# Compressed-branch scores: both parts of the keys as one 32-column operand, token tiles in two turns

## The chip, the cores and the metric

The kernel runs on one core of one Trainium2 chip. The metric is the device time of one execution in microseconds (us). The kernel before was timed three times: 971.80, 973.91 and 974.85 us, median 973.91.

## The reference, cut to what matters

The reference is a model of two layers over 256 tokens of width 1024. Each layer has an attention part of two branches (A: dilated attention of 24 heads; B: attention of 8 query heads over 2 key heads in three ways) and a convolutional feed-forward part. The change touches one of the three ways of branch B, the attention over compressed keys:

```python
k_cmp = compress(b_kv[:, :, 0, 0], cmp_pos[l, 0], cmp_w1[l, 0], cmp_w2[l, 0])
k_cmp = apply_rope(rmsnorm(k_cmp, b_k_g[l, 0]), cos_c, sin_c)
...
s = jnp.einsum('bqhgd,bchd->bqhgc', qb, k_cmp, preferred_element_type=jnp.float32) * scale
valid = (cmp_end[None, :] <= t[:, None])[None, :, None, None, :]
s_m = jnp.where(valid, s, NEG)
m = jnp.max(s_m, axis=-1, keepdims=True)
e = jnp.where(valid, jnp.exp(s_m - m), 0.0)
p = e / jnp.maximum(jnp.sum(e, axis=-1, keepdims=True), TINY)
o_cmp = jnp.einsum('bqhgc,bchd->bqhgd', p.astype(v_cmp.dtype), v_cmp)
...
o = g[:, :, 0] * o_cmp + g[:, :, 1] * o_sel + g[:, :, 2] * o_win
```

Every query head has at most 16 compressed keys, so the scores of all 8 heads for one tile of 128 tokens are a 128x128 matrix.

## The kernel before, in words

The 256 tokens stand in two tiles of 128. All matmuls of the large projections are done in three passes on operands split into a high and a low part (`hi` and `lo`, both `float32r`): `hi`x`hi`, `hi`x`lo`, `lo`x`hi` (`mm3`, L289 to L292). The weights come from memory as a stream of units; for each half of a unit, SP loads `raw` (L208), ScalarE rounds it to `hi` (L238), and VectorE subtracts to get `lo` (L239). `hi` and `lo` have two buffers each, `raw` has five. So a 512-column matmul of L290 or L291 needs L238, and one of L292 needs L239.

In a layer's attention part the main stream on TensorE are the nine chunks of the A projection (`chunk_in`, L445) and eight units of the merge gates (`merge`, L948). After each group of 12 chunk matmuls (four k steps of three passes for one token tile) stands a `tick()` (L274): a turn, in which every side job that is under way goes on to its next `yield`. Side jobs are `job_a` (attention of branch A, four times), `job_b` (selected and window attention of branch B, eight times) and `job_cmp1` and `job_cmp2` (compressed keys and attention). So the program's order is: 12 wide matmuls, one step of every side job, 12 wide matmuls, and so on. The tile framework plans the order on each engine from this: an instruction that is ready can be placed ahead of earlier ones that wait. What stands on an engine in the end is seen in the trace, not in the text of the program.

`job_cmp2` (L836) starts when the last quarter of the hidden units is summed (in chunk 5). It makes the compressed keys, transposes them (L879) and splits them to `kf[:, 0]` and `kf[:, 1]`, the high and the low part (L881). In its next turn it takes one of four `pt` buffers (L885) and one of five PSUM tiles (L886) and does the scores (L887 to L892): for each of two token tiles and 8 heads two matmuls, one for either part of the keys, accumulated in PSUM. The stationary operand is the queries `qS[:, h % 2, h // 2, tok]` (128x128, high and low part on the partitions), the moving one 16 columns of `kf`. So each pair loads the same queries twice.

In the same turn VectorE adds the mask while it reads PSUM (L896), scales (L898), and the softmax follows (L900 to L910, its exponential on ScalarE, L902). A turn later the probabilities are transposed (L914) and the `pt` buffer is given back, then L926 multiplies with the values, L930 adds to the branch's sum, and the result `oTb` is the operand of the projection of branch B (L993), which comes after all chunks and four merge units.

L571 and L576 in the trace are `job_a`: products of probabilities and values (`col_pair`, 64 columns of the array each) and transposes of probabilities (`transposed`). L706 and L614 are its work on VectorE. L864 is `job_cmp2`'s second compression product, L957 to L959 are the matmuls of `merge`.

Of the kernel before, what the change touches and what calls it, by code (L numbers as in the profile page):

```python
# [15 lines left out]
ALU = mybir.AluOpType  # L16
# [3 lines left out]
P = 128  # L20
# [144 lines left out]
def block_kernel(ctx, tc, x_in, xo_in, ws, g_norm, g_rope, pos, w2, conv, rope_c, ropec_c, mask_c, misc_c, out):  # L165
    nc = tc.nc
    V, A, G, T = nc.vector, nc.scalar, nc.gpsimd, nc.tensor
# [5 lines left out]
    def acc():  # L173
        t = acc_p.tile([P, 512], F32, name="acc")
        return t

    def att():
        t = att_p.tile([P, 512], F32, name="att")
        return t
# [14 lines left out]
    cmask = misc[:, 0:32].rearrange("p (t c) -> p t c", t=2)  # L194
# [180 lines left out]
    def attention_layer(l, pool, hT):  # L375
# [26 lines left out]
        qS = pool.tile([P, 2, 4, S], F32R, name="qS")  # L402
# [181 lines left out]
        def take(tag, n):  # L584
            while free[tag] < n:
                yield
            free[tag] -= n
# [227 lines left out]
        def w1_unit(w):  # L815
            while len(Fc) < 2:
                tick()
            if w == 0:
                hps["ps"] = att()
            ps = hps["ps"]  # L820
            for jp, half in enumerate(next_unit()):
                wv = half.rearrange("p (u v n) -> p u v n", u=2, v=2)
                for kv in range(2):
                    for u in range(2):
                        r = 64 * kv + 32 * u
                        jj = 4 * w + 2 * jp + u
                        T.matmul(ps[r:r + 32, 0:256], hps["F"][:, kv, jj].rearrange("p h c -> p (h c)"), wv[:, u, kv],
                                 start=jj < 2, stop=jj >= 14)
            if w < 3:
                return  # L830
            hid = pool.tile([P, 256], F32, name="hid", bufs=1)
            A.copy(hid, ps[:, 0:256])
            hps["hid"] = hid
            side.appendleft(job_cmp2())

        def job_cmp2():  # L836
            while ready["b"] < 6:
                yield
            ps = att()
# [21 lines left out]
            ps = att()  # L861
# [16 lines left out]
            ps = att()  # L878
            T.transpose(ps[:, :P], t1.rearrange("p a d -> p (a d)"), ident)  # L879
            kf = pool.tile([P, 2, P], F32R, name="kf", tag="hid", bufs=1)  # L880
# [3 lines left out]
            yield  # L884
            yield from take("pt", 1)  # L885
            ps = att()  # L886
            for t in range(2):  # L887
                tok = slice(t * P, (t + 1) * P)
                for h in range(8):
                    for i in range(2):  # L890
                        T.matmul(ps[:, t * P + h * 16:t * P + h * 16 + 16], qS[:, h % 2, h // 2, tok],
                                 kf[:, i, h * 16:(h + 1) * 16], start=i == 0, stop=i == 1)  # L892
            es = pool.tile([P, 16, 16], F32, name="es", tag="pt", bufs=4)
            e4 = es.rearrange("p (t h) c -> p t h c", t=2)
            for t in range(2):
                V.tensor_tensor(e4[:, t], ps[:, t * P:(t + 1) * P].rearrange("p (h c) -> p h c", h=8),  # L896
                                cmask[:, t, None, :].to_broadcast([P, 8, 16]), op=ALU.add)
            V.tensor_tensor(es, es, qscB.rearrange("p t h -> p (t h)")[:, :, None].to_broadcast([P, 16, 16]), op=ALU.mult)  # L898
            sm = pool.tile([P, 3, 16], F32, name="sm")
            V.tensor_reduce(sm[:, 0], es, axis=AX.X, op=ALU.max)  # L900
# [21 lines left out]
            for i in range(2):  # L922
                p3 = att()
                for j in range(2):
                    hp = 2 * i + j
                    T.matmul(p3[:, j * S:(j + 1) * S], vcb[:, 2 * hp:2 * hp + 2].rearrange("p h d -> p (h d)"), eT,  # L926
                             start=True, stop=True)
# [45 lines left out]
        for ab in "ba":  # L973
# [3 lines left out]
            for u in range(2):  # L977
# [9 lines left out]
                for mp in range(2):  # L987
                    ps = acc()
# [168 lines left out]
```

## Time and profile before

| what | value |
|---|---|
| three runs | 971.80, 973.91, 974.85 us |
| the profiled execution | 974.93 us, of which the span of the trace is 973.1 |
| TensorE matmul row (PE) | 949.1 us busy, 98% |
| TensorE weight loads (PEld) | 860.4 us, 88% |
| VectorE (DVE) | 753.5 us, 77% |
| ScalarE (ACT) | 580.7 us, 60% |
| GpSimd (POOL) | 156.4 us, 16% |
| mean granted TensorE clock | 0.992 |
| read from memory | 163.69 MB, 169 GB/s over the span |

Times in the rows are microseconds from the span's start, if not marked as ns. A matmul's duration in the trace holds its way through the pipeline; what a matmul costs in a dense stream is the distance from one start to the next. The granted clock is the share of TensorE's full clock (1.00 is 2.4 GHz, 0.50 is 1.2 GHz). L891 is a line of the program, and "acc<-lo,hT" says which tiles an instruction writes and reads.

### The profile page before, as it was taken

How to read it: one execution, taken by the hardware profiler on the slowest of the kernel's cores; microseconds unless marked ns; L12 is line 12 of the kernel's file. 1: busy time of each engine (PE TensorE's matmuls, PEld its weight loads, DVE VectorE, ACT ScalarE, POOL GpSimd, SP SyncE). 2: the span in 40 equal slices, each digit the busy share in tenths (PEclk: the TensorE clock that was granted, in tenths of full speed). 3: DMA queues.
4: the chain of work that ended last, by engine and by line, in shares of the span. 5: the costliest groups of instructions: out<-in, count | busy, mean ns of one | idle time of the engine just before them, and what ended most of it. 6: DMA issues, size and time to landing. Idle time of an engine off the chain costs nothing.

```text
span 973.1 us, 18637 instructions
## 1 busy us (share of the span) xinstructions
PE 949.1 (98%) x7154; PEld 860.4 (88%) x7154; DVE 753.5 (77%) x1593; ACT 580.7 (60%) x1186; POOL 156.4 (16%) x179
## 2 busy tenths in 40 slices
PE   6899999999999999999998999999999999999998
PEld 4778887878999999999986787877799999999998
DVE  6898866778669898986478987677876888998742
ACT  5778665667546555555456886565756565555431
POOL 5140211212003111110122301121300111111100
PEclk9999999999999999999999999999999999999999
DMA  7734447424456566565455344554354465666660
GB/s 234 258 132 153 152 152 219 172 87 143 146 173 213 175 202 201 182 195 199 160 166 174 111 150 135 197 189 131 106 195 150 148 229 173 197 196 197 200 209 22
DMA packets 48041, 165.95 MB, mean 171 GB/s; under 512 B 6096, under 2 KB 7632, under 8 KB 47824
## 3 DMA queue, kind: packets, MB, share of 16 engines
q1 hardware_dynamic: 46800, 163.71, 51.3%
q8 instruction: 56, 0.92, 0.4%
q10 hardware_dynamic: 1152, 1.05, 0.3%
q14 instruction: 33, 0.27, 0.1%
HBM read 163.69 MB, written 1.05 MB: 169 GB/s over the span
## 4 chain that ended last, share of the span: by engine, by line
PE 80%; DVE 10%; ACT 6%; issue 2%; DMA 1%; POOL 1%; SPq 0%; DVEq 0%; ACTq 0%; POOLq 0%
PE acc L373 25%; PE acc L290 6%; PE acc L292 6%; PE acc L291 6%; PE acc L1084 4%; DVE lo L239 4%; PE acc L1083 4%; PE acc L1082 4%; PE att L571 3%; PE acc L957 3%; PE acc L959 3%; PE acc L958 3%; PE att L576 2%; ACT pt L664 2%; PE acc L993 2%
## 5 line engine op out<-in xcount | busy, mean ns | idle before, releaser
L239 DVE TENSOR_TENSOR lo<-raw,hi 128x1024 fp32r<-128x1024 f32 (+1 forms) x292 | 368.0, 1278 | 54.7 <-ACT hi L238 51.7
L238 ACT CAST hi<-raw 128x1024 fp32r<-128x1024 f32 (+1 forms) x292 | 293.8, 1037 | 161.1 <-PE acc L291 41.3
L373 PE MATMUL acc<-u,hi 128*128 128x256 f32 x1376 | 237.7, 278 | 0.0
L373 PEld LDWEIGHTS acc<-u,hi 128*128 128x128 f32 x1376 | 208.2, 188 | 0.1
L373 PE MATMUL acc<-u,lo 128*128 128x256 f32 x688 | 190.9, 277 | 0.0
L290 PE MATMUL acc<-hi,hT 128*128 128x512 f32 (+1 forms) x384 | 156.1, 406 | 8.1 <-ACT hi L238 8.1
L292 PE MATMUL acc<-lo,hT 128*128 128x512 f32 (+1 forms) x384 | 152.3, 397 | 4.9 <-DVE lo L239 4.8
L291 PE MATMUL acc<-hi,hT 128*128 128x512 f32 (+1 forms) x384 | 150.1, 391 | 0.0
L373 PEld LDWEIGHTS acc<-u,lo 128*128 128x128 f32 x688 | 129.3, 188 | 0.0
L1083 PE MATMUL acc<-act,hi 128*128 128x256 f32 x352 | 97.4, 277 | 0.0
L1084 PE MATMUL acc<-act,lo 128*128 128x256 f32 x352 | 97.4, 277 | 0.0
L1082 PE MATMUL acc<-act,hi 128*128 128x256 f32 x352 | 97.3, 277 | 0.0
L290 PEld LDWEIGHTS acc<-hi,hT 128*128 128x128 f32 x384 | 74.0, 193 | 26.1 <-ACT hi L238 10.2
L292 PEld LDWEIGHTS acc<-lo,hT 128*128 128x128 f32 x384 | 73.9, 192 | 24.2 <-DVE lo L239 9.4
L291 PEld LDWEIGHTS acc<-hi,hT 128*128 128x128 f32 x384 | 74.2, 193 | 12.8 <-issue 0.3
L957 PE MATMUL acc<-hT,hi 128*128 128x256 f32 x256 | 73.3, 286 | 0.0
L959 PE MATMUL acc<-hT,lo 128*128 128x256 f32 x256 | 71.8, 280 | 0.2 <-DVE lo L239 0.2
L958 PE MATMUL acc<-hT,hi 128*128 128x256 f32 x256 | 71.7, 280 | 0.0
L1084 PEld LDWEIGHTS acc<-act,lo 128*128 128x128 f32 x352 | 66.1, 188 | 0.0
L1082 PEld LDWEIGHTS acc<-act,hi 128*128 128x128 f32 x352 | 66.1, 188 | 0.0
L1083 PEld LDWEIGHTS acc<-act,hi 128*128 128x128 f32 x352 | 66.1, 188 | 0.0
L1054 POOL TENSOR_TENSOR z<-z,rb 128x512 f32<-128x512 f32 x22 | 30.4, 1384 | 204.7 <-DVE z L1053 204.7
(214 smaller groups left out, 1705.4 us busy)
## 6 DMA issues: line engine op xcount, KB each, us to landing
raw<-in_ws_dram SPq DMA_DIRECT2D x300, 512.0 KB, 4.6
raw<-in_ws_dram SPq DMA_DIRECT2D x8, 280.0 KB, 4.6
x<-in_x_dram SPq DMA_DIRECT2D x1, 1024.0 KB, 9.5
out_dram<-x ACTq DMA_DIRECT2D x8, 128.0 KB, 2.4
gr<-in_g_rope_dram SPq DMA_DIRECT2D x2, 384.0 KB, 4.7
masks<-in_mask_dram SPq DMA_DIRECT2D x1, 576.0 KB, 7.5
xo<-in_xo_dram SPq DMA_DIRECT2D x2, 256.0 KB, 4.6
xo<-in_xo_dram SPq DMA_DIRECT2D x1, 512.0 KB, 7.5
```

Source lines behind the costliest of these rows:

```text
L238: A.copy(h, r)
L239: V.tensor_sub(l, r, h.bitcast(F32))
L290: T.matmul(o, a_hi, b_hi, start=first, stop=False)
L291: T.matmul(o, a_lo, b_hi, start=False, stop=False)
L292: T.matmul(o, a_hi, b_lo, start=False, stop=last)
L373: return [lambda a=a: T.matmul(a[0], a[1], a[2], start=a[3], stop=a[4]) for a in todo]
L957: T.matmul(o, hi[:, k, ms], hT[:, 0, k], start=k == 0, stop=False)
L958: T.matmul(o, hi[:, k, ms], hT[:, 1, k], start=False, stop=False)
L959: T.matmul(o, lo[:, k, ms], hT[:, 0, k], start=False, stop=k == 7)
L1082: T.matmul(ps, hi[:, c], act[:, 0, k], start=k == 0, stop=False)
L1083: T.matmul(ps, hi[:, c], act[:, 1, k], start=False, stop=False)
L1084: T.matmul(ps, lo[:, c], act[:, 0, k], start=False, stop=k == NFT - 1)
```

## The change

The two matmuls of a head become one: the moving operand is both parts of the keys, 2x16 columns, and the results land in two halves of the PSUM tile instead of being accumulated. After each token tile's eight matmuls the job yields, so that the score matmuls stand in two turns and the work of VectorE on them in a third. VectorE adds the second half in an instruction of its own.

```diff
             ps = att()
+            pv = ps.rearrange("p (i t h c) -> p i t h c", i=2, t=2, h=8)
             for t in range(2):
                 tok = slice(t * P, (t + 1) * P)
                 for h in range(8):
-                    for i in range(2):
-                        T.matmul(ps[:, t * P + h * 16:t * P + h * 16 + 16], qS[:, h % 2, h // 2, tok],
-                                 kf[:, i, h * 16:(h + 1) * 16], start=i == 0, stop=i == 1)
+                    T.matmul(pv[:, :, t, h], qS[:, h % 2, h // 2, tok], kf[:, :, h * 16:(h + 1) * 16], start=True, stop=True)
+                yield
             es = pool.tile([P, 16, 16], F32, name="es", tag="pt", bufs=4)
             e4 = es.rearrange("p (t h) c -> p t h c", t=2)
             for t in range(2):
-                V.tensor_tensor(e4[:, t], ps[:, t * P:(t + 1) * P].rearrange("p (h c) -> p h c", h=8),
-                                cmask[:, t, None, :].to_broadcast([P, 8, 16]), op=ALU.add)
+                V.tensor_tensor(e4[:, t], pv[:, 0, t], cmask[:, t, None, :].to_broadcast([P, 8, 16]), op=ALU.add)
+            V.tensor_tensor(e4, e4, pv[:, 1], op=ALU.add)
```

## Rows read from the trace of the kernel before

**Rows 1.** The page, part 1: busy time, share and instructions of each engine.

```profile
PE 949.1 (98%) x7154; PEld 860.4 (88%) x7154; DVE 753.5 (77%) x1593; ACT 580.7 (60%) x1186; POOL 156.4 (16%) x179
```

**Rows 2.** Windows: stretch and its length, then columns as the head line says.

```profile
core 0: us, PE busy (x) PEld busy (x) DVE busy (x) ACT busy (x) POOL busy (x), PEclk, DMA share, GB/s
176.60:187.50 10.90, 10.52 (x67) 8.13 (x66) 10.31 (x22) 7.74 (x17) 3.36 (x4) 1.00 0.57 189
...
187.50:209.70 22.20, 22.20 (x118) 18.18 (x116) 15.39 (x43) 9.26 (x25) 1.77 (x2) 0.85 0.28 94
...
190.46:197.27 6.81, 6.81 (x29) 5.69 (x29) 4.00 (x12) 0.83 (x2) 0.00 (x0) 0.50 0.31 116
...
671.74:675.14 3.40, 3.40 (x16) 2.59 (x13) 2.66 (x8) 0.68 (x2) 0.00 (x0) 0.50 0.37 127
...
197.30:232.00 34.70, 34.46 (x189) 26.98 (x189) 27.62 (x86) 25.07 (x67) 9.23 (x11) 1.00 0.30 105
```

**Rows 3.** Line L891: its matmuls (ns min/median/max), and who waited for it.

```profile
L891 PE MATMUL att<-kf,qS x64: 255/257/363, 187.6 to 671.2; 128*128 128x16 f32 x64
...
  DVE es L896: 5.0, 2
```

**Rows 4.** Timeline of layer 0: start us, us, engine, line, what, [idle before].

```profile
186.84 2.35 DVE L239 TENSOR_TENSOR lo<-raw,hi 128x1024 fp32r<-128x1024 f32 x2
...
187.59 4.38 PE L891 MATMUL att<-kf,qS 128*128 128x16 f32 x32
...
191.90 1.55 PE L571 MATMUL att<-pT,vA 128*64 128x128 f32 x12
192.01 0.49 DVE L896 TENSOR_TENSOR es<-att,misc 128x128 f32<-128x128 f32 x2 [2.82 <-PE att L891]
...
193.38 0.80 PE L292 MATMUL acc<-lo,hT 128*128 128x512 f32 x1
...
197.57 0.39 PE L290 MATMUL acc<-hi,hT 128*128 128x512 f32 x1
...
200.10 0.39 PE L292 MATMUL acc<-lo,hT 128*128 128x512 f32 x1
...
200.49 0.41 PE L914 MATMUL att<-ident,es 128*128 128x128 f32 x2
```

**Rows 5.** Timeline of layer 1, the same place.

```profile
667.74 3.72 PE L891 MATMUL att<-kf,qS 128*128 128x16 f32 x32
...
676.16 0.40 PE L290 MATMUL acc<-hi,hT 128*128 128x512 f32 x1
```

**Rows 6.** Timeline of TensorE in other places of layer 0, at full clock.

```profile
227.14 1.09 PE L571 MATMUL att<-pT,vA 128*64 128x256 f32 x12
228.16 0.88 PE L576 MATMUL att<-ident,pt 128*128 128x128 f32 x6
228.79 0.48 PE L290 MATMUL acc<-hi,hT 128*128 128x512 f32 x1
229.10 0.39 PE L291 MATMUL acc<-hi,hT 128*128 128x512 f32 x1
...
179.64 1.04 PE L864 MATMUL att<-w2t,hr 128*128 128x64 f32 x8
...
171.69 0.28 PE L958 MATMUL acc<-hT,hi 128*128 128x256 f32 x1
...
172.72 0.28 PE L958 MATMUL acc<-hT,hi 128*128 128x256 f32 x1
```

**Rows 7.** Lines L896 and L706 on VectorE, ns min/median/max.

```profile
L896 DVE TENSOR_TENSOR es<-att,misc x4: 279/286/292, 192.0 to 671.7; 128x128 f32<-128x128 f32 x4
...
L706 DVE TENSOR_TENSOR res<-att,sc x8: 413/420/426, 143.6 to 753.2; 128x256 f32<-128x256 f32 x8
```

**Rows 8.** Timeline: the first matmul of branch B's projection in layer 0.

```profile
232.53 0.39 PE L993 MATMUL acc<-oTb,hi 128*128 128x256 f32 x1
```

**Rows 9.** Waits of TensorE from 20 to 330: us in total, times, longest.

```profile
PE acc L292 <- DVE lo L239: 3.4, 4, 2.2
```

## The prediction

> **What bounds the kernel now.** I read the busy shares first. TensorE's matmul row is busy for 98% of the span, VectorE for 77%, ScalarE for 60% [rows 1]. A row near 100% is not proof, since matmul ends are modelled, so I went on to start-to-start distances in the timeline: outside the places named below, TensorE starts its 512-column matmuls every 0.230 us for tens of us (from 197.57 to 200.10 are 11 distances) [rows 4]. The kernel is bound by TensorE's instruction stream, and VectorE's `lo` parts of the weights follow close behind.
>
> Then I asked where the changed line stands. It is 64 matmuls in all, 32 a layer, each 128x16 with a full 128x128 weight load of its own [rows 3]. In the timeline of layer 0 they start at 187.59 and the next thing (L571) at 191.90; VectorE stands 2.82 us at L896 for them [rows 4], 5.0 us in both layers [rows 3]. The stretches show more: the granted clock is 0.50, the lower of the two levels (1.2 instead of 2.4 GHz), from 190.46 to 197.27 and from 671.74 to 675.14, and 1.00 afterwards [rows 2]. What TensorE did just before either fall is this block of 16-column matmuls. After the fall the ten distances from the 512-column L292 at 193.38 to 197.57 take 4.19 us, 0.42 each, against 0.230 at full clock [rows 4]. So the block costs twice: by its loads, and by the half clock of the useful matmuls behind it.
>
> **The change part by part.**
>
> *Matmuls.* 32 a layer become 16, with 32 columns each. Distance now: 0.112 us (L891's 32 cover 4.38 us in layer 0, the end of them slowed, and 3.72 in layer 1: (3.72 - 0.26)/31 = 0.112) [rows 3, 5]. No row has 32 columns with this load. Eight matmuls of 64 columns (L864) cover 1.04 us, 0.11 each, and nine distances of 256-column matmuls with the same load (L957 to L959) take 1.03 us, 0.114 each [rows 6]. From 16 to 256 columns the distance is the same, so the load sets it; between 0.11 and 0.114 I take 0.112, 16 x 0.112 = 1.79 us a layer. That a wider operand makes it less than 0.11 is excluded by the same rows.
>
> *The block and what follows, at full clock.* Layer 0 now: from 187.59 to the L290 at 197.57, 9.98 us [rows 4]. The same work with 16 matmuls and the clock at 1.00: 1.79, then L571 x12 in 1.02 (227.14 to the next start at 228.16), then the ten distances of 512-column matmuls, the first at 0.31 (228.79 to 229.10) and nine at 0.230, 2.38 [rows 6]. Sum 5.19, saved 4.79. Layer 1 now: 667.74 to 676.16, 8.42 us [rows 5], saved 3.23. Together 8.02 us, of which 3.58 is the 32 matmuls fewer and 4.44 the clock. The second turn costs two more resumptions of the 512-column stream at some 0.1 (0.31 against 0.23): 0.2. Left 7.8.
>
> *Does the clock stay up?* The change leaves 16 instead of 32 thin matmuls and means to put ordinary ones between the two eights. But the order on TensorE is not the program's: in layer 0 the L571 of the same turn, and L891, stand ahead of ten 512-column matmuls of the turn before, which waited for the `lo` that VectorE makes from 186.84 to 189.19 [rows 4]. The eights of both turns could be pulled together in the same way. Even then the thin stretch is 1.8 us, while the clock fell 2.9 us (layer 0) and 4.0 us (layer 1) after the block's start [rows 2, 4, 5]. I take it that the clock holds in both layers.
>
> A rule speaks against this. The neighbours of the thin block are transposes (L576) and the 64-wide L571. In this trace such a stretch by itself (L571 and L576 from 227.14 to 228.79) lies in a window whose granted clock is 1.00 [rows 2, 6]. The Trainium skill, in "TensorE: Matmul & The Clock Gate", Part 4 (PE-mode transpose), says that a transpose doesn't count for the clock gate as a matmul does. By that, transposes before and after the eights would lengthen the quiet stretch, and the clock could fall again; that would be the first rival below, at 971.5.
>
> *VectorE.* L896 keeps its size (0.29 x2). The new add reads 128x256 from PSUM, like L706: 0.42 a layer, 0.84 in all (bounds: 0.29 as for half the elements, 0.42) [rows 7]. It is hidden: VectorE is busy for 15.39 of the 22.2 us from 187.5 to 209.7 [rows 2], and the 2.82 us in which it stood for L891 go, because the scores are read two turns later. Without that cover it is 0.84 us.
>
> *What moves.* The chain from L896 to the transposes L914 and the products L926 comes two turns later. A turn of 12 matmuls is 12 x 0.230 = 2.8 us, so 5 to 6 us. Its consumer, the first L993, starts at 232.53, 32 us behind L914 at 200.49 [rows 4, 8]: nothing waits. One of four `pt` slots and one of five PSUM tiles are held two turns longer; the next job needs two `pt`. The chain issues no DMA; SP's weight loads wait for L239 and move forward with it, at a DMA share of 0.57 or less there [rows 2].
>
> *The new wait.* L896 now waits for the second turn's matmuls. Behind it in VectorE's queue are L239 (the `lo` parts), on which the 512-column L292 depends. VectorE had 22.2 us for its 15.39 in this stretch; with 4.8 us less and 0.42 more it is 15.8 of 17.4, 91%. Just before, VectorE was busy for 10.31 of 10.9 us, and TensorE for 10.52 [rows 2], so such density costs little. Bounds: nothing, and one wait a layer as long as the longest of L292 for L239 in layer 0, 2.2 us [rows 9]. Below nothing it can go too: if what VectorE stood for (5.0 us) was ending last somewhere, up to half of it, 2.5, comes on top. I take 0.5 a layer, nearer the dense stretch than the longest wait: 1.0.
>
> **Sum.** 8.0 - 0.2 - 1.0 = 6.8 us. The profiled execution took 974.93 (span 973.1, 1.8 around it): 968.1 us. It is 1.0 above the median 973.91 of three runs from 971.8 to 974.85; half-clock stretches of varying length would make such a spread, and a changed kernel without them doesn't depend on it. Against the median the gain is 5.8 us, 0.6%. A change under 0.3% (2.9 us) can't be told from none.
>
> **Rivals.**
>
> *The clock falls again.* The two eights are drawn together between L576 and L571, and each layer still has one stretch of the shorter length, 3.40 us at 0.50 [rows 2], which loses half of it, 1.7 us. 968.1 + 3.4 = 971.5; in one layer alone, 969.8. For it: the order on TensorE [rows 4], and layer 1, where the clock fell when the block was already over. Against: half the thin time. Chance 0.16.
>
> *TensorE's gain turns into waits for VectorE.* TensorE comes 4 us earlier to L292 and stands there for L239. The longest wait, 2.2, in place of 0.5 in each layer: 968.1 + 3.4 = 971.5. For it: VectorE at 91%. Against: VectorE loses its own stand, and TensorE ran at 10.52 of 10.9 beside a VectorE at 95%. Chance 0.12.
>
> *Slower: VectorE's queue is held by the later scores.* If L896 is placed ahead of an L239 that the 512-column matmuls between the two turns need, VectorE stands until the second eight, and the score chain, ten instructions a layer between L896's 0.29 for 128 elements and L706's 0.42 for 256 [rows 7], 2.9 to 4.2 in all, runs before that `lo`; TensorE would stand for up to 4.2 + 2.8 = 7.0 us a layer. 974.9 - 7.8 + 14.0 = 981.1. It decides from 3.9 us a layer, where the gain is gone. For it: L896 stands today at the head of VectorE's queue for 2.82. Against: L891 overtook other work today, so the scores would be ready early rather than late. Chance 0.06.
>
> **How the numbers follow.** Forecast 0.66, with its own range 965.0 to 970.4 (2.5 us of VectorE's stand on top; the largest wait in one layer and some). The range over all goes down to 964.6 and up to 972.2, which takes in both rivals at 971.5 and leaves out the slower one. Faster: the forecast's 0.66 and some half of the two rivals at 971.5, which in one layer alone stay below 971.0: 0.79. Same: the rest of them, 0.14. Slower: 0.07, the third rival and 0.01 for a reordering that I don't see.
>
> **What would show it.** L891 with 32 instead of 64 matmuls at 0.112 apart; a granted clock of 1.00 in the stretches where it was 0.50; L896 no longer idle behind L891; the 512-column distances at 0.230 right behind the block. If the clock row shows 0.50 again, the first rival holds. If L292 waits for L239 by 2 us behind the block, the second. If VectorE idles at L896 behind L891 with L239 after it, the third. The forecast is wrong above 971.0.

## The result and the profile after

The changed kernel takes 966.57 us (median of six runs, 964.59 to 969.94) against 973.57 for the kernel before beside it (six runs, 971.61 to 975.94). The ratio is 0.994, with a 95% interval from 0.9923 to 0.9957: 4.2 to 7.5 us faster, 5.8 in the middle. The forecast was 968.1, 5.8 below the median that was known then.

The profiled execution of the changed kernel took 964.59 us, its span is 962.8. Part 1 of its page, as [rows 1]:

```profile
PE 936.6 (97%) x7122; PEld 848.9 (88%) x7122; DVE 753.0 (78%) x1595; ACT 580.2 (60%) x1186; POOL 154.7 (16%) x179
```

TensorE has 32 matmuls fewer (7122 instead of 7154). Its line L891, which answers to [rows 3] (ns min/median/max):

```profile
L891 PE MATMUL att<-kf,qS x32: 262/263/283, 186.6 to 663.8; 128*128 128x32 f32 x32
...
who waited for it (us, times):
```

There are 32 matmuls of 32 columns, and the list of who waited for them is empty, where VectorE had waited 5.0 us. The timeline of layer 0, TensorE and VectorE, beside [rows 4]:

```profile
186.61 1.04 PE L891 MATMUL att<-kf,qS 128*128 128x32 f32 x8
187.58 0.88 PE L571 MATMUL att<-pT,vA 128*64 128x128 f32 x12
188.39 1.06 PE L891 MATMUL att<-kf,qS 128*128 128x32 f32 x8
...
189.30 0.48 PE L292 MATMUL acc<-lo,hT 128*128 128x512 f32 x1
189.49 0.49 DVE L896 TENSOR_TENSOR es<-att,misc 128x128 f32<-128x128 f32 x2
...
190.35 0.41 DVE L897 TENSOR_TENSOR es<-es,att 128x256 f32<-128x256 f32 x1
...
191.69 0.49 PE L544 MATMUL att<-ident,t 128*128 128x128 f32 x3
...
191.93 0.48 PE L290 MATMUL acc<-hi,hT 128*128 128x512 f32 x1
...
197.89 0.41 PE L914 MATMUL att<-ident,es 128*128 128x128 f32 x2 [0.29 <-DVE es L910]
...
226.93 0.39 PE L993 MATMUL acc<-oTb,hi 128*128 128x256 f32 x1
```

The same place of layer 1, beside [rows 5]:

```profile
661.22 1.04 PE L891 MATMUL att<-kf,qS 128*128 128x32 f32 x8
...
663.00 1.07 PE L891 MATMUL att<-kf,qS 128*128 128x32 f32 x8
...
666.54 0.48 PE L290 MATMUL acc<-hi,hT 128*128 128x512 f32 x1
```

From the first L891 to the L290 that stands ten wide matmuls behind the L292 after the block are now 5.32 us in both layers (186.61 to 191.93, 661.22 to 666.54), where it was 9.98 and 8.42: 4.66 and 3.10 us less, 7.76 together. Three transposes (L544, 0.24 us to the next start, 0.24 in layer 1 too) have moved into this stretch, which stood behind L914 before; without them 8.24 us are gone. The two eights (the eight matmuls of either token tile) are not separated by wide matmuls: both stand ahead of L292, with only L571 between them. VectorE reads the scores at 189.49, not later than before but earlier, and without idle time before it. The windows over the two blocks and behind each, beside [rows 2] (columns as the head line says):

```profile
core 0: us, PE busy (x) PEld busy (x) DVE busy (x) ACT busy (x) POOL busy (x), PEclk, DMA share, GB/s
186.50:189.30 2.80, 2.80 (x32) 2.60 (x31) 2.50 (x4) 0.86 (x2) 0.00 (x0) 1.00 0.46 114
189.30:193.00 3.70, 3.70 (x20) 3.05 (x20) 2.70 (x8) 1.51 (x4) 0.00 (x0) 1.00 0.58 220
...
661.20:663.90 2.70, 2.70 (x31) 2.50 (x30) 2.40 (x4) 0.83 (x2) 0.00 (x0) 1.00 0.46 147
663.90:667.50 3.60, 3.60 (x19) 3.00 (x19) 2.72 (x8) 1.40 (x4) 0.00 (x0) 1.00 0.54 199
```

The granted clock is 1.00 in and behind both blocks. The waits of TensorE from 20 to 330, as [rows 9], show no new wait for `lo`, but a small one for the end of the softmax (L910):

```profile
PE acc L292 <- DVE lo L239: 3.5, 4, 2.2
...
PE att L914 <- DVE es L910: 0.3, 1, 0.3
```

The two spans differ by 10.3 us, 2.5 more than the two blocks. The rest lies where nothing was changed: 0.98 before the first block, 0.88 between that L290 of layer 0 and the block of layer 1, 0.7 behind. One pair of executions doesn't tell these from chance: 52 executions of the kernel before, in all comparisons below, go from 968.48 to 977.48 us. So the experiments were read by medians and by the mean granted clock that each execution reports.

### The profile page after: what moved, and what is told of

It reads as the page before. It is cut to its first block, busy times and chain, and to the rows that moved or that the text cites. A ratio compares the mean times of both kernels' runs of the same rounds, so it can differ in the third digit from the quotient of the medians.

```text
span 962.8 us, 18575 instructions
## 1 busy us (share of the span) xinstructions
PE 936.6 (97%) x7122; PEld 848.9 (88%) x7122; DVE 753.0 (78%) x1595; ACT 580.2 (60%) x1186; POOL 154.7 (16%) x179
## 4 chain that ended last, share of the span: by engine, by line
PE 78%; DVE 10%; ACT 6%; issue 2%; POOL 1%; DMA 1%; SPq 0%; DVEq 0%; ACTq 0%; POOLq 0%
PE acc L373 25%; PE acc L290 5%; PE acc L292 5%; PE acc L291 5%; DVE lo L239 4%; PE acc L1082 4%; PE acc L1084 4%; PE acc L1083 4%; PE acc L957 3%; PE att L571 3%; PE acc L959 3%; PE acc L958 3%; PE att L576 2%; PE acc L993 2%; PE acc L994 2%
## 5 line engine op out<-in xcount | busy, mean ns | idle before, releaser
L290 PE MATMUL acc<-hi,hT 128*128 128x512 f32 (+1 forms) x384 | 154.0, 401 | 8.7 <-ACT hi L238 8.7
L292 PE MATMUL acc<-lo,hT 128*128 128x512 f32 (+1 forms) x384 | 150.0, 391 | 5.2 <-DVE lo L239 5.1
L291 PE MATMUL acc<-hi,hT 128*128 128x512 f32 (+1 forms) x384 | 148.5, 387 | 0.0
L290 PEld LDWEIGHTS acc<-hi,hT 128*128 128x128 f32 x384 | 72.6, 189 | 25.9 <-ACT hi L238 11.1
L292 PEld LDWEIGHTS acc<-lo,hT 128*128 128x128 f32 x384 | 72.4, 189 | 23.6 <-DVE lo L239 9.2
L291 PEld LDWEIGHTS acc<-hi,hT 128*128 128x128 f32 x384 | 72.7, 189 | 12.6 <-issue 0.3
```

Of the source, the lines that this page charges most:

```text
L290: T.matmul(o, a_hi, b_hi, start=first, stop=False)
L291: T.matmul(o, a_lo, b_hi, start=False, stop=False)
L292: T.matmul(o, a_hi, b_lo, start=False, stop=last)
```

## The experiments

Theory: 3.6 us are the 32 loads that are gone, the rest is the clock, which no longer falls behind a block half as long; VectorE's work is hidden. Rivals: the two turns do it; or the clock costs nothing that counts; or VectorE's freed queue gives the gain.

**One turn.** The change without its `yield`:

```diff
                     T.matmul(pv[:, :, t, h], qS[:, h % 2, h // 2, tok], kf[:, :, h * 16:(h + 1) * 16], start=True, stop=True)
-                yield
```

> The change without its two turns: 16 matmuls of 32 columns in one turn, VectorE's adds in the same turn. Theory (half from 16 fewer loads a layer, 1.8 us, half from the clock that no longer falls): the thin stretch is 1.8 us without a break, and the clock holds in most executions; against the kernel before 5 to 7 us faster, as the whole change is, within 1 us of it. Rival (it is the splitting in two turns that keeps the clock up): the granted clock falls to 0.50 behind the block in both layers, and only the loads are gained, 2.5 to 3.6 us.

Measured: 965.82 us, ratio 0.9929 (0.991 to 0.9949). The 16 matmuls stand without a break in its timeline:

```profile
186.90 1.94 PE L891 MATMUL att<-kf,qS 128*128 128x32 f32 x16
188.77 0.88 PE L571 MATMUL att<-pT,vA 128*64 128x128 f32 x12
189.58 0.50 PE L292 MATMUL acc<-lo,hT 128*128 128x512 f32 x1
```

Its granted clock there is 1.00. From the first L891 to L292 are 2.68 us, where the change with its two turns has 2.69 (186.61 to 189.30). The whole gain is there without the second turn, so the turns don't make it.

**Turns only.** The kernel before with 32 matmuls of 16 columns, but a `yield` after each token tile:

```diff
                                  kf[:, i, h * 16:(h + 1) * 16], start=i == 0, stop=i == 1)
+                yield
```

> The kernel before with its 32 matmuls of 16 columns a layer, but a yield after each token tile: 16 and 16, VectorE's adds in the third turn. Theory: the loads stay (32 x 0.112), and the thin stretches are 1.8 us each with L571 between; the clock falls as before in at least one layer, so 0 to 2 us faster than the kernel before, from VectorE's wait of 5.0 us in all that goes. Rival (the turns keep the clock up): the granted clock is 1.00 at both blocks and the kernel is 4 us faster.

Measured: 974.13 us, ratio 1.0012 (0.9998 to 1.0027): no gain, where 0 to 2 us were expected. VectorE's wait for L891 (L897 is its line here) is shorter in its profile than the 5.0 us of before, so relieving VectorE of most of it gains nothing by itself:

```profile
  DVE es L897: 1.7, 2
```

The windows of its profile hold a surprise (the first is the two blocks with L571 between, the last two are places where TensorE had waited for the sum of squares of the second norm, L344):

```profile
187.70:192.20 4.50, 4.50 (x47) 4.31 (x46) 2.65 (x4) 1.25 (x3) 0.00 (x0) 1.00 0.62 174
...
313.12:316.52 3.40, 3.40 (x19) 3.40 (x18) 2.82 (x5) 1.81 (x2) 0.42 (x1) 0.50 0.73 245
790.98:794.38 3.40, 3.40 (x19) 3.40 (x18) 2.38 (x7) 1.99 (x2) 0.70 (x1) 0.50 0.78 249
```

In this execution the clock held at the blocks, against what the theory expected, and fell in two other places and in the start. The mean clock over its twelve executions is 0.9936, that of the kernel before 0.9933. So where the clock falls changes from execution to execution, and one profile of a kernel doesn't settle it.

**Wide operand.** The kernel before with its 32 loads, each moving operand being all 256 columns of the keys:

```diff
-                        T.matmul(ps[:, t * P + h * 16:t * P + h * 16 + 16], qS[:, h % 2, h // 2, tok],
-                                 kf[:, i, h * 16:(h + 1) * 16], start=i == 0, stop=i == 1)
+                        T.matmul(ps[:, 0:S], qS[:, h % 2, h // 2, tok],
+                                 kf.rearrange("p i c -> p (i c)"), start=i == 0, stop=i == 1)
```

> The kernel before with 32 matmuls and 32 loads a layer, but each moving operand is all 256 columns of the keys instead of 16 (the scores are left out: each product overwrites the last). Same order on every engine. Theory: the load sets the distance, so the block still takes 32 x 0.112 to 0.114 = 3.6 us, but the granted clock stays 1.00: 4.4 us faster than the profiled execution of before, 3.4 to 5.1 in the medians. Rival (the clock costs nothing that counts, or doesn't hang on the thin block): same time as before within 1 us, or 0.50 behind the block again.

Measured: 970.82 us, ratio 0.9971 (0.9957 to 0.9985): 1.5 to 4.2 us faster with the same number of loads, 2.5 in the medians, less than the 3.4 to 5.1 expected. From its timeline, and its windows over the first block and behind it:

```profile
186.58 4.04 PE L891 MATMUL att<-kf,qS 128*128 128x256 f32 x32
```

```profile
186.58:190.55 3.97, 3.97 (x35) 3.83 (x34) 1.60 (x2) 0.81 (x2) 0.00 (x0) 1.00 0.53 163
190.55:197.40 6.85, 6.61 (x40) 5.23 (x40) 5.96 (x21) 3.53 (x8) 0.69 (x1) 1.00 0.17 65
```

The clock is 1.00 behind the block, its mean over eleven executions 0.9978 instead of 0.9933. Nothing else was changed but the columns that TensorE works on, so the thin block is what lets the clock fall more often. Its profile still has a fall at 518.96, behind a wait of TensorE for VectorE (L485 for L482, 1.81 us). The block itself became longer, (4.04 - 0.28)/31 = 0.121 a matmul instead of 0.112, 0.6 us in both layers, which the theory's upper end of 0.114 had missed.

**The change again, twice.** Without an edit, each time beside the kernel before on the same chip.

> The change as it is, beside the others on one chip. Theory: 5.8 to 7.5 us faster than the kernel before; block to tenth wide distance 5.3 us in either layer; granted clock 1.00 at both blocks. Rival (the clock still falls at the blocks in some executions, which would be the spread of 964.6 to 969.9 us): executions with a mean granted clock of 0.993 to 0.996 have their stretch at 0.50 behind L891.

> The change as it is, a third time, beside the next kernel: more executions for the mean of its granted clock (0.9965 over twelve, against 0.9983 over twelve of the one-turn form). If two turns make falls at or near the blocks more frequent: mean clock 0.996 to 0.997, median 966.5 to 967.5. If the difference was chance: mean clock 0.9975 to 0.9985, median 965.5 to 966.3.

Measured: 967.60 us, ratio 0.9942 (0.9921 to 0.9964), and 967.96 us, ratio 0.9937 (0.9924 to 0.995). The second set's mean clock, 0.9972, lies between its two forecasts, and its median above both. Neither profile has a fall at a block. The first has one at 25.67, in the start, the second at 27.85 and at 311.15. The last, by its windows and timeline:

```profile
307.70:311.10 3.40, 1.85 (x17) 1.84 (x17) 2.71 (x5) 1.70 (x3) 0.61 (x1) 1.00 0.52 163
311.16:314.56 3.40, 3.40 (x18) 3.40 (x17) 2.82 (x5) 1.41 (x2) 0.03 (x1) 0.50 0.70 223
```

```profile
309.26 0.61 PE L344 MATMUL att<-ones,fin 128*128 128x1 f32 x4 [1.55 <-DVE fin L333]
```

TensorE was busy for 1.85 of 3.40 us, waiting for L333 and then doing L344's one-column matmuls, and the clock fell behind that. So the rival of the first of these two, that the falls which are left stand behind L891, is not borne out; where they lie in executions without a trace stays unseen.

**Double loads.** The one-turn form with every matmul issued twice:

```diff
+                    for _ in range(2):
-                    T.matmul(pv[:, :, t, h], qS[:, h % 2, h // 2, tok], kf[:, :, h * 16:(h + 1) * 16], start=True, stop=True)
+                        T.matmul(pv[:, :, t, h], qS[:, h % 2, h // 2, tok], kf[:, :, h * 16:(h + 1) * 16], start=True, stop=True)
```

> The change in one turn with every one of its matmuls issued twice: 32 loads a layer again, of 32 columns, with the same order as the kernel before. Theory: the 3.6 us of the loads come back, and a thin stretch of 3.6 us without a break brings the clock's falls back: median 972 to 974, within 1.5 us of the kernel before, mean granted clock near 0.994; set to equal clock by 0.67 us for each 0.001 (the slope over 64 executions) within 0.7 us of the kernel before. Rival (twice the columns of before keep the clock up): mean clock 0.998, median 969 to 970.

Measured: 973.26 us, ratio 1.0003 (0.9985 to 1.0021), mean clock 0.9936. The whole gain is gone. In its profile, timeline and window of layer 1 (L892 is the score line here), the fall behind the block is back; at the block of layer 0 the clock held:

```profile
663.62 4.26 PE L892 MATMUL att<-kf,qS 128*128 128x32 f32 x32
667.81 1.55 PE L571 MATMUL att<-pT,vA 128*64 128x128 f32 x12
```

```profile
666.61:673.43 6.82, 6.82 (x29) 5.62 (x29) 3.36 (x9) 0.40 (x1) 0.00 (x0) 0.50 0.27 96
```

**Extra adds.** The change with four more instructions on VectorE behind the new one:

```diff
-            V.tensor_tensor(e4, e4, pv[:, 1], op=ALU.add)
+            [V.tensor_tensor(e4, e4, pv[:, 1], op=op) for op in (ALU.add, ALU.subtract, ALU.add, ALU.subtract, ALU.add)]
```

> The change with four more instructions on VectorE behind the new add (subtract and add the second half again, twice): 4 x 0.41 = 1.65 us more a layer, 3.3 in all. Theory (VectorE's work there is hidden beside TensorE): 0 to 1 us slower than the change, 4.5 to 7 us faster than the kernel before. Rival (VectorE is the next bound in this stretch, so the new add cost its 0.84 and the clock gave more): 2.5 to 3.3 us slower than the change.

Measured: 966.86 us, ratio 0.993 (0.9905 to 0.9954), as the change itself. The five stand in VectorE's timeline:

```profile
191.56 2.23 DVE L897 TENSOR_TENSOR es<-es,att 128x256 f32<-128x256 f32 x5
194.72 0.29 DVE L437 TENSOR_TENSOR t<-qraw,tabs 128x128 f32<-128x128 f32 x1 [0.93 <-ACT qraw L419]
```

Even behind them VectorE idles 0.93 us. Its work is hidden in this stretch, apart from the 0.3 us at L914 that the change has in each layer.

**Trailing heads.** Each head's product also runs over the keys of the heads behind it, whose own products then write the right values there; once in one turn, once with the change's two turns:

```diff
-                    T.matmul(pv[:, :, t, h], qS[:, h % 2, h // 2, tok], kf[:, :, h * 16:(h + 1) * 16], start=True, stop=True)
+                    T.matmul(pv[:, :, t, h:8], qS[:, h % 2, h // 2, tok],
+                             kf[:, :, h * 16:].rearrange("p i (h c) -> p i h c", c=16), start=True, stop=True)
```

> The change in one turn, with a wider operand at the same number of loads: head h's product also runs over the keys of the heads behind it (2 x (8-h) x 16 columns, 32 to 256, 144 on average), and the next heads write the right values over them. Theory (the load sets the distance, width is free and keeps the clock up): block 16 x 0.112 to 0.121 = 1.8 to 1.94 us a layer, mean granted clock 0.998 to 1.000, median 965 to 966, 7 to 8 us faster than the kernel before and at most 1 us faster than the change. Rival (32 columns already keep the clock up and width costs, as 256 columns took 0.121 instead of 0.112): same clock as the one-turn kernel, 0 to 0.5 us slower than that.

> The change with both turns kept and the wider operand (each head's product runs over the heads behind it as well, 144 columns on average, same 16 loads, same order). If the falls that are left in the change come from its thin eights: mean clock 0.998 or more, median 965 to 966, at or below the change by 1 us. If they come from other places: mean clock as the change beside it, within 0.001, and the same time within 0.7 us.

Measured: 966.08 us, ratio 0.9926 (0.9902 to 0.9951), and 966.02 us, ratio 0.9931 (0.9917 to 0.9944). The block of the first:

```profile
187.25 1.95 PE L891 MATMUL att<-kf,qS 128*128 128x256 f32 x16
```

At 144 columns on average a distance is (1.95 - 0.26)/15 = 0.113: here width is free. The mean clock is 0.9980 in both, as in the one-turn form with 32 columns (0.9983). Neither is told from the change by its interval. Of the two forecasts for the form in two turns the clock fits both, and the time, 966.02 against 967.96 beside it, rather the first, that the thin eights let the clock fall; yet no traced fall stands behind them, so this is open.

**One turn again.**

> The one-turn form again, to see whether its clock (0.998 on average over six executions against 0.9965 over twelve of the change) is its own. Theory (order makes no difference: the loads decide, the falls of the clock that are left come by chance elsewhere): mean clock 0.9955 to 0.998, median 965.5 to 967.5. Rival (the break into two turns makes falls more frequent): mean clock 0.998 again, median at or under 966.

Measured: 965.81 us, ratio 0.9928 (0.9902 to 0.9953), mean clock 0.9983 over both sets: the rival's numbers. The forms in one turn are lower than the change by some 1 us in the median and by 0.0016 in the clock, but the change with the extra adds, which has two turns, stands at 0.9977. Whether the break into two turns makes falls more frequent is not settled.

**All executions together.** Each execution reports its time and its mean granted clock. A line was fitted through the 135 of them, with one level for each kernel and a common slope: 0.68 us for each 0.001 of mean clock (standard error 0.05). The level is the time at a clock of 1.000:

| kernel | executions | median | mean clock | level at 1.000 |
|---|---|---|---|---|
| before | 52 | 973.41 | 0.9933 | 968.7 ± 0.4 |
| turns only | 12 | 974.12 | 0.9936 | 969.8 ± 0.5 |
| double loads | 12 | 973.26 | 0.9936 | 969.0 ± 0.5 |
| wide operand, 32 loads | 11 | 970.82 | 0.9978 | 969.0 ± 0.3 |
| the change | 17 | 967.00 | 0.9967 | 965.2 ± 0.3 |
| the change, extra adds | 7 | 966.86 | 0.9977 | 965.1 ± 0.4 |
| one turn | 12 | 965.82 | 0.9983 | 965.1 ± 0.3 |
| trailing heads, one turn | 6 | 966.09 | 0.9980 | 964.8 ± 0.4 |
| trailing heads, two turns | 6 | 966.02 | 0.9980 | 965.0 ± 0.4 |

The ± is one standard error. The executions come from two chips; the kernel before has levels of 968.6 and 968.4 on the one and 968.9 on the other.

The levels fall into two groups, and the number of loads tells them apart: 968.7 to 969.8 with 32 loads a layer, 964.8 to 965.2 with 16. That turns only stands 1.1 above the kernel before (standard error 0.3) isn't explained; its profile has TensorE waiting 1.0 us in all for the softmax (L915 for L911), which the profile before doesn't have, but no run ties the two together. The common slope is a simplification: fitted by themselves, the three kernels with 32 thin matmuls a layer have 0.82 ± 0.07, the six others 0.51 ± 0.07. With these two slopes the kernel before is at 967.7 and the change at 965.8, 2.0 apart instead of 3.5. A comparison that needs no line is wide operand (mean 970.46 us at a clock of 0.9978) against the two forms with trailing heads (966.23 at 0.9980): 4.2 us, standard error 0.5, where the distances of their blocks make it 64 x 0.121 - 32 x 0.113 = 4.1.

The clocks fall into two groups as well, and the length of the thin block tells them apart: 0.9933 to 0.9936 with 32 thin matmuls, 0.9967 to 0.9983 with 16, or with 32 wide ones. The traces say the same of the blocks: with 32 thin matmuls 3 of 6 have a fall behind them (before 2 of 2, double loads 1 of 2, turns only 0 of 2), all others 0 of 18.

## Why the prediction was right

**The loads.** Forecast 32 x 0.112 = 3.58 us. In the profile the matmuls of an eight are (1.04 - 0.26)/7 = 0.111 us apart, and wide operand against trailing heads, at nearly the same clock, differ as their distances say. The levels of before and after differ by 968.7 - 965.2 = 3.5 with the common slope, by 2.0 with two. The term was right, as far as the runs tell. One row beside it was misread: the 1.02 us for L571 are of a place where it has 256 columns; behind the block it has 128 and took 0.81.

**The clock.** Forecast: it holds in both layers, 4.44 us. The mechanism is right: the clock is 1.00 at both blocks of the changed kernel's profile, width alone brings it back with 32 loads, and doubled matmuls take it away again. The size was off. Over all executions the mean clock goes from 0.9933 to 0.9967, which at 0.68 us for each 0.001 is 2.3 us; with the two slopes 3.8 of the 5.8 us are the clock's. Two things were missed. The working took it that both blocks have their fall in every execution: 0.0034 of mean clock on 972 us are 6.6 us less at half clock, where the profile had 10.2 behind the blocks. Falls in other places, in the start and behind L344, happen in some executions and stay. And it priced the half clock by two places where TensorE had dense work, 4.44 of 10.2 us, 0.43. Over all executions 0.001 of mean clock is 1.94 us at half clock and costs 0.68, or 0.35. If some falls meet a TensorE that waits anyway, it would come out so; that isn't shown.

**The order.** It was feared that both eights would be drawn ahead of the wide matmuls. They were, and L571 alone stands between them; the one-turn form shows that it doesn't matter for the loads, and not visibly for the clock. The Trainium skill, in "TensorE: Matmul & The Clock Gate", Part 4 (PE-mode transpose), says that a transpose doesn't count for the clock gate as a matmul does. By that rule a fall was to be feared here, with the transposes L576 right before the eights; the window from 186.50 to 189.30 has 1.00, and so has the one behind it, so the rule did not decide. (The prediction also spoke of transposes behind the eights; what stood there was L571, which are products.) The 0.2 us for the second turn did not come: the two turns did not break the stream of wide matmuls a second time, and 2.69 us to L292 are as good as the 2.68 of the one-turn form.

**VectorE.** The new add takes 0.41 and is hidden, as forecast, but for a wait that no term had: TensorE's matmuls stand 0.29 us at L914 for L910 (0.30 in layer 1), a wait that the profile before doesn't have. The 1.0 us set aside for waits for `lo` did not come: L292 waits 3.5 us in all from 20 to 330 instead of 3.4, and four more instructions a layer leave the level where it was (965.1 against 965.2). The third rival's mechanism, VectorE held by the later scores, did not come about: L896 starts without idle time. That the score chain would be two turns later held in the program and not on the engine; L914 started 2.6 us earlier than before by the clock on the trace, 197.89 instead of 200.49, and L993 still comes 29 us behind it.

**The sum.** 3.58 + 4.44 - 0.2 - 1.0 = 6.8 was forecast against the profiled execution, and 5.8 against the median. Measured: 5.8, by the ratio and by the means of 52 and 17 executions alike. That the two agree is luck. Loads and clock together came out 2.2 short of their 8.0; and the 0.2 for the second turn and the 1.0 of waits did not come, which, with the 1.0 that the profiled execution lay above the median, makes 2.2 as well. The two profiled executions differ by 10.3, not 6.8. The time itself came out 1.5 below the forecast. The lower end of the forecast's own range, 965.0, doesn't follow from the 2.5 us named for it (968.1 - 2.5 = 965.6); the measured 966.57 lies above both.

## What to carry to other kernels

- A small matmul costs its weight load, here one of 128x128: 0.112 us whether 16 or 32 columns follow, and 0.113 at 144 on average. Count loads, and let everything that shares a stationary operand ride on one.
- A run of thin matmuls can cost as much again behind it, when the granted clock falls and the next wide matmuls go at half speed (0.42 us apart instead of 0.230). It doesn't in every execution, so one profile can show the fall or miss it. Read the clock of the window behind a block, not only the block; an operand that is wider than needed is a cheap test.
- Where a time varies between executions, set each execution's time against its mean clock; what is left at equal clock belongs to the change, as far as one slope holds for both kernels. Two kernels with the same mean clock need no slope.

## What the runs showed of the hardware that was not expected

- The place of a fall changes between executions of one program: the kernel before fell at both blocks and in the start (26.61) in its profile, the turns-only kernel at neither block, but in the start and at 313.11 and 790.97, the change in three profiles once at 311.15, otherwise only in the start and at the very end, and the one-turn form once at 636.19, behind a wait of L621 for ScalarE.
- Equal loads are not quite equal in distance: 32 matmuls of 256 columns took 0.121 us each, where 16 of 144 columns on average took 0.113, and 256-column products in the merge units 0.114 [rows 6]. What makes 0.121 was not tried.
